# Another order of the tokens inside each 128 of the prompt, for a decoder layer with a state-space half and a gated half

## The chip, the cores and the metric

The kernel runs on one core of one Trainium2 chip. The metric is the device time of one execution in microseconds (us); the kernel before takes 1127.18 us (median of 3 runs, 1125.74 to 1130.81). Engines: TensorE (PE in the rows, PEld its weight loads), VectorE (DVE), ScalarE (ACT), GpSimd (POOL) and SyncE (SP, which only issues transfers here). Every engine works through its own list of instructions in order.

## The reference, cut to what matters

One layer for 1024 prompt tokens and 8 x 8 sample tokens (NT = 1088), width 1024:

```python
h = rmsnorm(x, norm1)
p = h @ w_in                                  # 512 columns for S5, 2 x 512 for the chunk mixer
# S5: per group of 16 channels a diagonal complex state of 64, scanned over the tokens
y = Re(C h_t) + d_skip * xf;  g = gelu(y)
o_s5 = g * sigmoid(g @ w_glu + b_glu)
# chunk mixer: inside each 128 tokens out = gelu(u) * (tril(w_s) @ layernorm(gelu(v)) + b_s)
mix = concat(rmsnorm(o_s5, g_s5), rmsnorm(o_cm, g_cm))
x = x + mix @ w_out
x = x + (silu(n @ w_gate) * (n @ w_up)) @ w_down   # n = rmsnorm(x, norm2)
y_out = rmsnorm(x, norm_f)
```

Outputs are also the last states and the normed v rows of the last chunk. All of it is in fp32.

## The kernel before, in words

Activations stand with channels on the 128 partitions and tokens along the free axis. fp32 products are made from pairs: a value x is split into a high part xh (ScalarE copies and rounds it, line 140) and a low part xl (VectorE subtracts, line 141; function `split`), and `mm3` issues three matmuls for one product. Tokens are worked in three chunks, `CH`: 384, 384 and 320 (256 of the prompt and the 64 sample tokens). The stages in time:

- **0 to 80 us**: x comes in, norm1 is summed, and `s5_in` makes the S5 input: matmuls `pu`, then line 287 multiplies them by the norm factor rB and writes them to a tile US of shape [128, 8, 136], that is [channel, t, c] where token n is c = n // 8, t = n % 8. Consecutive tokens thus lie 136 words apart: the view `tc2n` turns [p, t, c] round to [p, c, t], a step of 136 words at every element. US goes to DRAM (us_d), from where the S5 groups read it.
- **80 to 226 us**: S5, eight iterations, each with matmuls and small transfers of its state (Sw, gw, mb); between them the matmuls of the chunk mixer (`pv`, `pu`, `spt`) fill TensorE. Each iteration writes its result to DRAM (ys_d).
- **226 to 291 us**: the GLU. ys_d is read back into four tiles g ([128, 8, 136], line 742, `G5`). `s5_act` splits g into xh and xl for the matmuls (through `tc2n`: source with a step of 136 words), `glu` has matmuls `pg`, a sigmoid sg on ScalarE, the product g * sg in place on VectorE (line 762, step of 136), its square on ScalarE (lines 174 and 179) and the running sum of squares (line 180). `glu_mix` sums over the partitions with a matmul against ones (`ss`, line 158), takes the reciprocal root (`rsqrt_bc`: ScalarE line 165, VectorE lines 166 to 168), scales g (line 699) and splits it once more. It runs once per chunk; the output product `po` of the other half (the chunk mixer's) lies around it, two of the three `glu_mix` being placed behind the 6th and 11th of its 16 groups.
- **291 to 330 us**: the second half of the output product. Then the norm and the first sums of the feed-forward part, **420 to 835 us** its gate and up matrices, **835 us on** its down matrix and the last norm.

The sums `ss` have one bank of PSUM of their own (tag `sp`), so each sum waits until VectorE has read the one before with line 166. The pool `raw` has three buffers, through which all weights from DRAM go before they are split (function `load_q`, line 227); a load is issued when a buffer is free. The order of instructions on every engine is decided by a scheduler when the program is built.

Of the kernel before, what the change touches and what calls it, by code (L numbers as in the profile page):

```python
# [13 lines left out]
AF = mybir.ActivationFunctionType  # L14
# [4 lines left out]
D = 1024  # L19
# [3 lines left out]
NF = 22  # L23
CH = ((0, 384), (384, 384), (768, 320))
# [58 lines left out]
def layer_kernel(ctx: ExitStack, tc: tile.TileContext, A, O, dbg=None):  # L83
# [37 lines left out]
    def tc2n(a, n0, n):  # L121

        return a[:, :, n0 // 8:(n0 + n) // 8].rearrange("p t c -> p c t")

    def nat(a):
        return a.rearrange("p (c t) -> p c t", t=8)
# [43 lines left out]

    def accum_sq(pl, acc, src, first):

        if first:
            S.activation(acc, src, AF.Square)
            return
        sq = tmp_sq(pl, int(np.prod(src.shape[1:])), "sq")
        if len(src.shape) == 3:
            sq = nat(sq)
        S.activation(sq, src, AF.Square)
        V.tensor_tensor(acc, acc, sq, ALU.add)  # L180
# [99 lines left out]
    def s5_in(q, c):  # L280
        n0, n = CH[c]
        pp = fm_group(q, c, "s5" if c == 2 else "mm")
        for m in range(2):
            mt = 2 * q + m
            if c == 0:
                US[mt] = prep.tile([128, 8, 136], F32, tag="us", name="us", bufs=2)
            V.tensor_tensor(tc2n(US[mt], n0, n), nat(pp[m]), nat(rB[:, n0:n0 + n]), ALU.mult)  # L287
            if c == 2:
                Q.dma_start(fmaj(us_d, mt), US[mt])
# [360 lines left out]
    def cm_out(q, c):  # L650
# [3 lines left out]
        for i in range(2):  # L654
# [11 lines left out]
            for om, o, w in om_blocks(m, c):  # L666
                d = [x[:, o:o + w] for x in (p, ur, sqo[:, n0:n0 + n])]
                t_ = 128 if w > 64 else 8
                d = [x.rearrange("p (j t) -> p j t", t=t_) for x in d]
                om = om.rearrange("p (j t) -> p j t", t=t_) if w == 64 else om  # L670
                V.scalar_tensor_tensor(om, d[0], gcol("lng", m), bB[:, m:m + 1, 0:t_].to_broadcast([128, w // t_, t_]),
                                       op0=ALU.mult, op1=ALU.add)
                V.tensor_tensor(om, om, d[1], ALU.mult)
                if m == 0:
                    S.activation(d[2], om, AF.Square)
                    continue
                sq = tmp_sq(cwp, w, "sq").rearrange("p (j t) -> p j t", t=t_)
                S.activation(sq, om, AF.Square)
                V.tensor_tensor(d[2], d[2], sq, ALU.add)
# [64 lines left out]
    def s5_act(c):  # L744
        n0, n = CH[c]
        for m in range(4):
            split(tc2n(G5[m], n0, n), nat(xh[:, m, n0:n0 + n]), nat(xl[:, m, n0:n0 + n]))
# [3 lines left out]
    def glu(c):  # L751
        n0, n = CH[c]
        acc = ACC5[c] = gl.tile([128, 384], F32, tag="acc", name="acc", bufs=3)[:, :n]
        for m in range(4):
# [6 lines left out]
            z = tc2n(G5[m], n0, n)  # L761
            V.tensor_tensor(z, z, nat(sg), ALU.mult)
            accum_sq(gl, nat(acc), z, m == 0)

    def glu_mix(c):
        n0, n = CH[c]
        rb = rsqrt_bc(gl, sum_sq(ACC5[c], n), n, 1.0 / W)
        for m in range(4):
            scaled_split(tc2n(G5[m], n0, n), gcol("gs5", m), nat(rb), nat(xh[:, m, n0:n0 + n]),
                         nat(xl[:, m, n0:n0 + n]))  # L770
# [457 lines left out]

S5P = np.arange(512).reshape(4, 8, 16).transpose(0, 2, 1).reshape(-1)


def lay(inp):
# [3 lines left out]
    A = {"xT": xt.T.reshape(8, 128, NT).transpose(1, 0, 2)}  # L1236
# [33 lines left out]
    pos = np.arange(128)  # L1270
    ws, bs = one("w_s"), one("b_s")
    A["wsT"] = ws.transpose(2, 0, 1)
    tt, bb = np.tile(np.arange(8), 8), np.repeat(np.arange(8), 8)
    A["bd"] = ws[:, tt][:, :, tt].transpose(2, 0, 1)
    mk = np.zeros((128, 192), np.int32)
    mk[:, :128] = pos[:, None] <= pos[None, :]
    mk[64:, 128:] = (tt[:, None] <= tt[None, :]) & (bb[:, None] == bb[None, :])
    A["mk"] = mk
    A["bB"] = bs.reshape(4, 2, 128).transpose(1, 0, 2)
# [6 lines left out]
def unlay(R):  # L1286
    y = R["yT"].reshape(D, NT).T
# [4 lines left out]
    cvp, cvs = R["cvp"].reshape(1, 1, 128, W), R["cvs"].reshape(1, 8, 8, W)  # L1292
# [18 lines left out]
```

## Time and profile before

| | |
|---|---|
| time, median of 3 runs | 1127.18 us (1125.74 to 1130.81) |
| profiled execution: time | 1127.69 us |
| its span, granted clock of TensorE | 1125.6 us, 0.982 |
| TensorE busy, weight loads busy | 1056.9 us (94%), 1029.3 us (91%) |
| VectorE, ScalarE, GpSimd busy | 907.8 us (81%), 449.4 us (40%), 316.3 us (28%) |

The profiled execution is one run of its own; its time is 2.1 us over its span (start and end outside the profile), and it lies 0.5 us over the median of the runs. Times inside it are counted from the start of the span. TensorE is the engine with the most work, so what an edit does to the time is read from TensorE's idle stretches and from what each of them waits for.

### The profile page before, as it was taken

The numbers are of one execution on the slowest core, as the hardware profiler recorded it, in microseconds if no ns is written. First come the engines' busy times: TensorE is split into PE (matmuls) and PEld (weight loads), VectorE is DVE, ScalarE is ACT, GpSimd is POOL, SyncE is SP. The second block draws the span as 40 slices with busy tenths as digits, with TensorE's granted clock in tenths as the row PEclk, the third lists the DMA queues.
The fourth block names the chain that finished last, engine by engine and source line by source line (L and its number), as shares of the span: only waits on it lengthen the run. The fifth ranks groups of instructions, "written<-read, shape, count | busy, mean of one in ns | idle before, by whom it ended". The sixth has DMA issues, their size and how long they took to land.

```text
span 1125.6 us, 20406 instructions
## 1 busy us (share of the span) xinstructions
PE 1056.9 (94%) x7966; PEld 1029.3 (91%) x7966; DVE 907.8 (81%) x1780; ACT 449.4 (40%) x822; POOL 316.3 (28%) x287
## 2 busy tenths in 40 slices
PE   7799999978899989999999999999999999999994
PEld 6789999868799879999999999999998899899994
DVE  6987999889999897667657656657668979879998
ACT  7314334398454442232232232233234324425561
POOL 5010330000000344334334334435434331223220
PEclk9989999989899899999999999999999999999998
DMA  8342334251533113223223223133156815514304
GB/s 272 106 116 74 96 114 153 76 181 43 192 102 101 50 56 127 69 95 127 69 95 126 68 97 125 57 108 126 57 186 213 291 38 184 179 52 135 130 16 158
DMA packets 81519, 131.19 MB, mean 117 GB/s; under 512 B 8976, under 2 KB 60048, under 8 KB 81296
## 3 DMA queue, kind: packets, MB, share of 16 engines
q1 hardware_dynamic: 81424, 129.91, 35.5%
q8 instruction: 62, 1.02, 0.4%
q14 instruction: 33, 0.27, 0.1%
HBM read 90.43 MB, written 34.24 MB: 111 GB/s over the span
## 4 chain that ended last, share of the span: by engine, by line
PE 68%; DVE 19%; DMA 6%; issue 4%; ACT 3%; POOL 1%; SPq 0%; DVEq 0%; ACTq 0%; POOLq 0%
PE u L146 16%; PE u L144 16%; PE u L145 16%; DMA h<-hid_d 4%; DVE xl L141 3%; PE pu L144 2%; PE pu L146 2%; PE pu L145 2%; PE po L146 2%; PE po L144 2%; PE po L145 2%; PE pv L145 2%; PE pv L146 2%; PE pv L144 2%; DVE cwr L141 1%
## 5 line engine op out<-in xcount | busy, mean ns | idle before, releaser
L144 PE MATMUL u<-xh,h 128*128 128x272 f32 x516 | 149.5, 290 | 1.9 <-ACT h L140 1.7
L146 PE MATMUL u<-xh,h 128*128 128x272 f32 x516 | 149.1, 290 | 1.3 <-DVE h L141 1.3
L145 PE MATMUL u<-xl,h 128*128 128x272 f32 x516 | 149.0, 289 | 1.2 <-DVE xl L141 1.2
L144 PE MATMUL u<-xh,fb 128*128 128x272 f32 x382 | 110.5, 289 | 0.6 <-DVE x1r L1108 0.4
L145 PE MATMUL u<-xl,fb 128*128 128x272 f32 x382 | 110.4, 289 | 0.6 <-DVE xl L141 0.6
L146 PE MATMUL u<-xh,fb 128*128 128x272 f32 x382 | 110.3, 289 | 0.2 <-DVE fb L141 0.2
L1023 POOL TENSOR_TENSOR tS<-q,q 128x512 f32<-128x512 f32 x22 | 29.1, 1321 | 262.3 <-DVE h L888 158.4
L144 PEld LDWEIGHTS u<-xh,h 128*128 128x128 f32 x516 | 97.4, 189 | 2.7 <-ACT h L140 2.1
L146 PEld LDWEIGHTS u<-xh,h 128*128 128x128 f32 x516 | 97.4, 189 | 1.9 <-DVE h L141 1.9
L145 PEld LDWEIGHTS u<-xl,h 128*128 128x128 f32 x516 | 97.5, 189 | 1.4 <-DVE xl L141 1.4
L140 ACT ACTIVATE h<-q 128x512 fp32r<-128x512 f32 (+1 forms) x83 | 51.1, 615 | 82.0 <-PE u L145 75.8
L144 PE MATMUL pu<-xh,cwr 128*128 128x384 f32 (+1 forms) x192 | 66.4, 350 | 9.0 <-DVE us L287 9.0
L141 DVE TENSOR_TENSOR h<-q,h 128x512 fp32r<-128x512 f32 (+1 forms) x83 | 68.7, 830 | 6.4 <-ACT h L140 5.3
L145 PEld LDWEIGHTS u<-xl,fb 128*128 128x128 f32 x382 | 72.3, 189 | 1.0 <-DVE xl L141 0.9
L144 PEld LDWEIGHTS u<-xh,fb 128*128 128x128 f32 x382 | 72.2, 189 | 1.0 <-DVE x1r L1108 0.6
L146 PEld LDWEIGHTS u<-xh,fb 128*128 128x128 f32 x382 | 72.0, 189 | 0.4 <-DVE fb L141 0.4
L1061 ACT ACTIVATE st<-st 128x272 f32<-128x272 f32 x88 | 37.8, 431 | 71.2 <-DVE st L1083 35.1
L145 PE MATMUL pu<-xl,cwr 128*128 128x384 f32 (+1 forms) x192 | 65.2, 341 | 0.0
L146 PE MATMUL pu<-xh,cwr 128*128 128x384 f32 (+1 forms) x192 | 65.1, 342 | 0.0
L140 ACT ACTIVATE fb<-q 128x512 fp32r<-128x512 f32 (+1 forms) x64 | 38.7, 607 | 61.2 <-PE u L145 48.3
L1028 POOL TENSOR_TENSOR tS<-tS,q 128x512 f32<-128x512 f32 x22 | 29.8, 1354 | 114.6 <-DVE h L141 61.3
L144 PE MATMUL u<-cwr,h 128*128 128x272 f32 x189 | 55.1, 292 | 1.6 <-ACT cwr L140 1.0
(439 smaller groups left out, 3765.7 us busy)
## 6 DMA issues: line engine op xcount, KB each, us to landing
hid_d<-st SPq DMA_DIRECT2D x22, 952.0 KB, 4.2
h<-hid_d SPq DMA_DIRECT2D x28, 544.0 KB, 3.9
q<-in_w_gate_dram SPq DMA_DIRECT2D x22, 512.0 KB, 3.5
q<-in_w_up_dram SPq DMA_DIRECT2D x22, 512.0 KB, 3.5
q<-in_w_d_dram SPq DMA_DIRECT2D x16, 512.0 KB, 3.9
wo<-in_w_out_dram SPq DMA_DIRECT2D x14, 512.0 KB, 4.2
wi<-in_w_in_dram SPq DMA_DIRECT2D x12, 512.0 KB, 4.9
h<-hid_d SPq DMA_DIRECT2D x14, 408.0 KB, 3.2
```

Source lines behind the costliest of these rows:

```text
L140: S.activation(hi, src, AF.Copy)
L141: return (eng or V).tensor_tensor(lo, src, hi.bitcast(F32), ALU.subtract)
L144: PE.matmul(p, wh, ah, start=start, stop=False)
L145: PE.matmul(p, wh, al, start=False, stop=False)
L146: return PE.matmul(p, wl, ah, start=False, stop=stop)
L1023: P.tensor_tensor(tS, a21, a22, ALU.add)
L1028: P.tensor_tensor(tS, tS, a11, ALU.subtract)
L1061: S.activation(dst, src, AF.Silu)
```

## The change

Inside each 128 tokens of the prompt the order becomes t first, then c: place 16 t + c holds token 8 c + t (c from 0 to 15, t from 0 to 7). The 64 sample tokens are turned in the same way (8 x 8). With that, 16 neighbouring tokens of the free axis lie in 16 neighbouring words of a [p, t, c] tile (8 for the sample tokens). The third chunk has both kinds, so `tc2n` returns a list of pieces: one for the first two chunks, two (256 and 64 tokens) for the third. The scaling in `glu_mix` becomes one instruction per 128 tokens. Mask, spatial matrices, biases, x and the outputs are permuted on the host. Sizes and number of transfers stay.

```diff
-    def tc2n(a, n0, n):
-
-        return a[:, :, n0 // 8:(n0 + n) // 8].rearrange("p t c -> p c t")
-
-    def nat(a):
-        return a.rearrange("p (c t) -> p c t", t=8)
+    def tc2n(a, n0, n, *rest):
+
+        out = []
+        for o, w in ((0, n),) if n0 + n < NT else ((0, n - 64), (n - 64, 64)):
+            c0, cc = ((n0 + o) // 8, 16) if w > 64 else (128, 8)
+            v_ = a[:, :, c0:c0 + w // 8]
+            e = "p (j t c) -> p j t c" if w > 64 else "p (t c) -> p t c"
+            if w > 64:
+                v_ = v_.rearrange("p t (j c) -> p j t c", c=16)
+            out.append([v_] + [x[:, o:o + w].rearrange(e, t=8, c=cc) for x in rest])
+        return out
...
+    SQT = {}
+
+    def accum_to(pl, acc, first):
+
+        SQT[0] = acc if first else tmp_sq(pl, acc.shape[1], "sq")
+        return SQT[0]
+
+    def accum_end(acc, first):
+        if not first:
+            V.tensor_tensor(acc, acc, SQT[0], ALU.add)
...
-            V.tensor_tensor(tc2n(US[mt], n0, n), nat(pp[m]), nat(rB[:, n0:n0 + n]), ALU.mult)
+            for us_, p_, r_ in tc2n(US[mt], n0, n, pp[m], rB[:, n0:n0 + n]):
+                V.tensor_tensor(us_, p_, r_, ALU.mult)
...
-            split(tc2n(G5[m], n0, n), nat(xh[:, m, n0:n0 + n]), nat(xl[:, m, n0:n0 + n]))
+            for x in tc2n(G5[m], n0, n, xh[:, m, n0:n0 + n], xl[:, m, n0:n0 + n]):
+                split(*x)
...
-            z = tc2n(G5[m], n0, n)
-            V.tensor_tensor(z, z, nat(sg), ALU.mult)
-            accum_sq(gl, nat(acc), z, m == 0)
+            for z, s_, q_ in tc2n(G5[m], n0, n, sg, accum_to(gl, acc, m == 0)):
+                V.tensor_tensor(z, z, s_, ALU.mult)
+                S.activation(q_, z, AF.Square)
+            accum_end(acc, m == 0)
...
-            scaled_split(tc2n(G5[m], n0, n), gcol("gs5", m), nat(rb), nat(xh[:, m, n0:n0 + n]),
-                         nat(xl[:, m, n0:n0 + n]))
+            for x in range(0, n, 128):
+                w = min(128, n - x)
+                z = G5[m][:, :, (n0 + x) // 8:(n0 + x + w) // 8]
+                r_ = rb[:, x:x + w].rearrange("p (t c) -> p t c", t=8)
+                V.scalar_tensor_tensor(z, z, gcol("gs5", m), r_, op0=ALU.mult, op1=ALU.mult)
+            for x in tc2n(G5[m], n0, n, xh[:, m, n0:n0 + n], xl[:, m, n0:n0 + n]):
+                split(*x)
...
+CP = np.arange(128).reshape(16, 8).T.reshape(-1)
+TP = np.concatenate([(128 * np.arange(8)[:, None] + CP).reshape(-1), 1024 + np.arange(64).reshape(8, 8).T.reshape(-1)])
...
-    A = {"xT": xt.T.reshape(8, 128, NT).transpose(1, 0, 2)}
+    A = {"xT": xt[TP].T.reshape(8, 128, NT).transpose(1, 0, 2)}
...
-    A["wsT"] = ws.transpose(2, 0, 1)
+    A["wsT"] = ws[:, CP][:, :, CP].transpose(2, 0, 1)
```

Since the scheduler sees other durations, it also puts instructions elsewhere. Three places. On SP, at the end of S5: ys_d is the last result written to DRAM, g the four loads back, wo weights of the output product, x1a the residual. Before:

```order
L573 DMA ys_d<-ys 128x544
L742 DMA g_2718<-ys_d 128x8x136
L742 DMA g_2720<-ys_d 128x8x136
L742 DMA g_2722<-ys_d 128x8x136
L742 DMA g_2724<-ys_d 128x8x136
L227 DMA wo_3007<-in_w_out_dram 128x1024
```

and now (line 227 has become 242, 573 has become 589, 742 has become 761):

```order
L589 DMA ys_d<-ys 128x544
L242 DMA wo_3035<-in_w_out_dram 128x1024
L761 DMA g_2722<-ys_d 128x8x136
L761 DMA g_2724<-ys_d 128x8x136
L761 DMA g_2726<-ys_d 128x8x136
L761 DMA g_2728<-ys_d 128x8x136
L242 DMA wo_3118<-in_w_out_dram 128x1024
```

A weight load that came behind the four g loads is now ahead of them. On TensorE, at the same time: ss sums the squares of the chunk mixer's output (sqo), spt is its spatial product, yb the last S5 iteration's output and pg the first GLU product. Before:

```order
L570 MATMUL yb<-Hp,QK 128x136
L158 MATMUL ss<-sqo,ones 128x384
L664 MATMUL spt<-wT,v 64x128 x4
L664 MATMUL spt<-bd,v 64x64 x2
L158 MATMUL ss<-sqo,ones 128x384
L144 MATMUL pg<-xh,wgh 128x384 x7
```

and now:

```order
L164 MATMUL ss<-sqo,ones 128x384
L585 MATMUL yb<-U,mb_833 128x136 x2
L680 MATMUL spt<-wT,v 64x128 x4
L680 MATMUL spt<-bd,v 64x64 x2
L164 MATMUL ss<-sqo,ones 128x384
L586 MATMUL yb<-Hp,QK 128x136
```

Both sums now stand ahead of the last yb matmuls instead of behind them. On VectorE, between the reading of the first and of the second sum of `glu_mix` (rsa): g is scaled (line 699, now 794), xl is its low part, cwr a split of weights, x1a and x1q take the output product's groups. Before:

```order
L168 SCALAR_TENSOR_TENSOR rsy<-rsa,rsy 128x384
L699 SCALAR_TENSOR_TENSOR g_2718<-g_2718,gp,rsy 128x48x8
L699 SCALAR_TENSOR_TENSOR g_2720<-g_2720,gp,rsy 128x48x8
L699 SCALAR_TENSOR_TENSOR g_2722<-g_2722,gp,rsy 128x48x8
L699 SCALAR_TENSOR_TENSOR g_2724<-g_2724,gp,rsy 128x48x8
L141 TENSOR_TENSOR cwr<-wo_3170,cwr 128x1024
L141 TENSOR_TENSOR xl<-g_2718,xh 128x384
L141 TENSOR_TENSOR xl<-g_2720,xh 128x384
L141 TENSOR_TENSOR xl<-g_2722,xh 128x384
L141 TENSOR_TENSOR xl<-g_2724,xh 128x384
L166 SCALAR_TENSOR_TENSOR rsa<-ss,rsy 128x384
```

and now:

```order
L174 SCALAR_TENSOR_TENSOR rsy<-rsa,rsy 128x384
L794 SCALAR_TENSOR_TENSOR g_2722<-g_2722,gp,rsy 128x8x16 x3
L794 SCALAR_TENSOR_TENSOR g_2724<-g_2724,gp,rsy 128x8x16 x3
L794 SCALAR_TENSOR_TENSOR g_2726<-g_2726,gp,rsy 128x8x16 x3
L794 SCALAR_TENSOR_TENSOR g_2728<-g_2728,gp,rsy 128x8x16 x3
L842 TENSOR_TENSOR x1a<-x1a,po 128x272
L147 TENSOR_TENSOR cwr<-wo_3118,cwr 128x1024
L842 TENSOR_TENSOR x1q_3049<-x1q_3049,po 128x272
L147 TENSOR_TENSOR xl<-g_2722,xh 128x384
L147 TENSOR_TENSOR xl<-g_2724,xh 128x384
L842 TENSOR_TENSOR x1q_3049<-x1q_3049,po 128x272
L147 TENSOR_TENSOR xl<-g_2726,xh 128x384
```

The block of scaling and splitting was unbroken and now has the output product's additions between its parts; the scalings are twelve instead of four. The low parts of the S5 stage's filler and its matmuls also stand in another mixture, with the same work.

## Rows read from the trace of the kernel before

**Rows 1.** The page's busy time of each engine, and instructions.

```profile
PE 1056.9 (94%) x7966; PEld 1029.3 (91%) x7966; DVE 907.8 (81%) x1780; ACT 449.4 (40%) x822; POOL 316.3 (28%) x287
```

**Rows 2.** Windows: stretch, length, busy us per engine (instructions), clock, DMA share, GB/s.

```profile
80.00:226.00 146.00, 144.80 (x1111) 134.88 (x1109) 134.99 (x303) 55.02 (x126) 24.29 (x29) 1.00 0.38 108
226.00:235.00 9.00, 2.21 (x16) 1.28 (x16) 5.89 (x11) 8.06 (x10) 0.00 (x0) 0.82 1.05 291
235.00:262.00 27.00, 25.35 (x139) 24.61 (x139) 26.61 (x43) 25.71 (x39) 0.00 (x0) 0.93 0.35 123
262.00:291.00 29.00, 20.88 (x149) 19.43 (x147) 27.89 (x58) 19.95 (x33) 0.00 (x0) 0.92 0.35 115
291.00:330.00 39.00, 37.63 (x288) 37.20 (x287) 36.83 (x72) 19.14 (x30) 0.00 (x0) 0.97 0.32 108
```

**Rows 3.** TensorE's timeline; in brackets the idle time before and what ended it.

```profile
56.76 0.66 PE L144 MATMUL pu<-xh,cwr 128*128 128x384 f32 x1 [6.99 <-DVE us L287]
69.87 0.38 PE L144 MATMUL pu<-xh,cwr 128*128 128x320 f32 x1 [1.97 <-DVE us L287]
...
222.21 0.70 PE L569 MATMUL yb<-U,mb 128*128 128x136 f32 x4 [1.16 <-DMA mb<-mb]
...
234.63 2.61 PE L144 MATMUL pg<-xh,wgh 128*128 128x384 f32 x7 [2.96 <-ACT xh L140]
...
256.94 0.81 PE L158 MATMUL ss<-sqo,ones 128*128 128x320 f32 x2 [1.34 <-DVE cwf L166]
267.66 0.91 PE L158 MATMUL ss<-acc,ones 128*128 128x384 f32 x2 [1.43 <-DVE cwf L166]
277.04 0.91 PE L158 MATMUL ss<-acc,ones 128*128 128x384 f32 x2 [1.29 <-DVE rsa L166]
289.91 1.44 PE L158 MATMUL ss<-acc,ones 128*128 128x320 f32 x2 [5.40 <-DVE rsa L166]
...
319.02 0.73 PE L158 MATMUL ss<-fbt,ones 128*128 128x272 f32 x2 [1.36 <-DVE fbt L874]
```

**Rows 4.** VectorE's groups of one shape: busy us, mean ns of one, idle before.

```profile
L141 DVE TENSOR_TENSOR xl<-g,xh 128x384 fp32r<-128x384 f32 x16 | 13.6, 896 | 0.0
...
L762 DVE TENSOR_TENSOR g<-g,sg 128x384 f32<-128x384 f32 x8 | 7.4, 934 | 0.4 <-ACT sg L760 0.4
L699 DVE SCALAR_TENSOR_TENSOR g<-g,gp,rsy 128x384 f32<-128x384 f32 x8 | 7.3, 992 | 0.0
L287 DVE TENSOR_TENSOR us<-pu,rB 128x384 f32<-128x384 f32 x8 | 6.5, 905 | 2.0 <-DMA us_d<-us 2.0
...
L657 DVE TENSOR_TENSOR cwf<-pu,rB 128x384 f32<-128x384 f32 x8 | 4.4, 544 | 0.1
L141 DVE TENSOR_TENSOR xl<-v,xh 128x384 fp32r<-128x384 f32 x8 | 4.2, 557 | 0.0
...
L608 DVE SCALAR_TENSOR_TENSOR cwf<-rB,idn 128x128 f32<-128x128 f32 x9 | 2.8, 307 | 0.1
```

**Rows 5.** VectorE's timeline in `glu_mix`.

```profile
281.68 3.59 DVE L699 SCALAR_TENSOR_TENSOR g<-g,gp,rsy 128x384 f32<-128x384 f32 x4
...
289.29 0.56 DVE L166 SCALAR_TENSOR_TENSOR rsa<-ss,rsy 128x384 f32<-128x384 f32 x1
```

**Rows 6.** TensorE's timeline behind the longest idle stretch.

```profile
291.37 0.43 PE L145 MATMUL po<-xl,fb 128*128 128x272 f32 x1
...
292.96 0.41 PE L146 MATMUL po<-xh,fb 128*128 128x272 f32 x1
...
293.84 0.29 PE L146 MATMUL po<-xh,cwr 128*128 128x272 f32 x1
293.96 0.29 PE L144 MATMUL po<-xh,cwr 128*128 128x272 f32 x1
```

**Rows 7.** SP's timeline at the g loads: start, time of the four issues.

```profile
226.65 4.53 SPq L742 DMA_DIRECT2D g<-ys_d  x4
```

**Rows 8.** DMA issues: KB each, median us from issue to landing.

```profile
Sw<-Ss SPq DMA_DIRECT2D x16, 128.0 KB, 2.7
```

More of the change, by code (lines that the diff above doesn't have):

```diff
@@ L176, in accum_sq @@
         sq = tmp_sq(pl, int(np.prod(src.shape[1:])), "sq")
-        if len(src.shape) == 3:
-            sq = nat(sq)
         S.activation(sq, src, AF.Square)
@@ L670, in cm_out @@
                 om = om.rearrange("p (j t) -> p j t", t=t_) if w == 64 else om
-                V.scalar_tensor_tensor(om, d[0], gcol("lng", m), bB[:, m:m + 1, 0:t_].to_broadcast([128, w // t_, t_]),
-                                       op0=ALU.mult, op1=ALU.add)
+                if w > 64:
+                    bias = bB[:, m:m + 1, :].to_broadcast([128, w // 128, 128])
+                else:
+                    bias = bB[:, m, 0:128:16].unsqueeze(2).to_broadcast([128, 8, 8])
+                V.scalar_tensor_tensor(om, d[0], gcol("lng", m), bias, op0=ALU.mult, op1=ALU.add)
                 V.tensor_tensor(om, om, d[1], ALU.mult)
@@ L1269, in lay @@
     A["ln"] = np.stack([one("cm_ln_g"), one("cm_ln_b")])
-    pos = np.arange(128)
     ws, bs = one("w_s"), one("b_s")
-    A["wsT"] = ws.transpose(2, 0, 1)
-    tt, bb = np.tile(np.arange(8), 8), np.repeat(np.arange(8), 8)
+    A["wsT"] = ws[:, CP][:, :, CP].transpose(2, 0, 1)
+    tt, bb = np.repeat(np.arange(8), 8), np.tile(np.arange(8), 8)
     A["bd"] = ws[:, tt][:, :, tt].transpose(2, 0, 1)
     mk = np.zeros((128, 192), np.int32)
-    mk[:, :128] = pos[:, None] <= pos[None, :]
+    mk[:, :128] = CP[:, None] <= CP[None, :]
     mk[64:, 128:] = (tt[:, None] <= tt[None, :]) & (bb[:, None] == bb[None, :])
     A["mk"] = mk
-    A["bB"] = bs.reshape(4, 2, 128).transpose(1, 0, 2)
+    A["bB"] = bs[:, CP].reshape(4, 2, 128).transpose(1, 0, 2)
     return {k: np.ascontiguousarray(x) for k, x in A.items()}
@@ L1286, in unlay @@
 def unlay(R):
-    y = R["yT"].reshape(D, NT).T
+    y = np.empty((NT, D), np.float32)
+    y[TP] = R["yT"].reshape(D, NT).T
     yp, ys = y[:1024].reshape(1, 1024, D), y[1024:].reshape(8, 8, D)
@@ L1291, in unlay @@
     ss = [fs[64 * i:64 * i + 64, :, 1:].transpose(2, 1, 0)[None] for i in range(2)]
-    cvp, cvs = R["cvp"].reshape(1, 1, 128, W), R["cvs"].reshape(1, 8, 8, W)
+    cvp = R["cvp"].reshape(1, 1, 8, 16, W).transpose(0, 1, 3, 2, 4).reshape(1, 1, 128, W)
+    cvs = R["cvs"].reshape(1, 8, 8, W).transpose(0, 2, 1, 3)
     return tuple(np.ascontiguousarray(x) for x in (yp, ys, sp[0], sp[1], cvp, ss[0], ss[1], cvs))
```

## Prediction

> **What bounds the kernel now.** I read the page's busy times first. TensorE is busy 94% of the span, VectorE 81%, ScalarE 40% [rows 1]; the change takes work from VectorE and ScalarE alone, so it can only give time where TensorE stands idle for them. Where that is, the windows show: in S5 TensorE is busy 144.80 of 146.00 us, while from 235 to 291 it is busy 25.35 + 20.88 = 46.23 of 56 us and VectorE 26.61 + 27.89 = 54.50 of 56 [rows 2]. In the GLU, then, VectorE sets the pace. TensorE's timeline tells which waits these are [rows 3]. Before the pu matmuls of the first stage it stands 6.99 and 1.97 us, both ended by line 287, which writes US. From 256.94 to 289.91 four sums (ss) find their one bank still unread: 1.34, 1.43, 1.29 and 5.40 us, together 9.46, ended by VectorE's line 166 each time. The longest ends at 289.91, when VectorE reaches line 166 at 289.29 [rows 5]; ahead of it in VectorE's list lay the scaling of g (four instructions, 3.59 us), a split of weights and four low parts of g. So the instructions that the change makes cheaper are the ones that the longest wait waits for.
>
> **The price of one instruction.** Strided and unstrided forms of the same size stand side by side in VectorE's groups [rows 4]:
> - line 287 (us from pu) 905 ns, against 544 for line 657, the same product from the same kind of tile to one without steps: 0.36 less.
> - xl from g 896, against xl from v 557: 0.34 less.
> - line 762 (g times sg) 934, against the same 544: 0.39 less.
> - line 699 (scaling g) 992. It becomes three instructions of 128x128; line 608 has that shape at 307, so three are 921. But neighbours overlap: four of line 699 take 3.59 us [rows 5] and not 4 x 0.992 = 3.97, which is 0.13 less at each of three joints. Three instructions thus stand at 0.921 - 2 x 0.13 = 0.66, so 0.3 less.
>
> The third chunk (320 tokens, in two pieces) gains less, from the same rows by estimate some 0.3, 0.25, 0.3 and 0.25 (size 320/384, and one more instruction). No row shows an instruction with runs of 16 words on a side that is written; I take it to be as fast as an unstrided one, the nearest row of the same work, and keep no gain at all as the other end.
>
> [...]
>
> **The terms, in order of time.**
> 1. *First stage.* TensorE goes on at 56.76 when the first instruction of a pair of line 287 has read its bank. Ahead of it in VectorE's list stands the first pair. Three instructions at 0.36 are -1.1. Nothing, if VectorE waits there for x anyway; six at 0.36, -2.2, if all that stand before 69.87 count.
> 2. *S5 in another mixture.* The same instructions, TensorE 99% busy: 0. Between -1 (the wait of 1.16 at 222.21 goes [rows 3]) and +2.5 (two more such).
> 3. *Start of the GLU.* A weight load of 512 KB now stands ahead of the g loads on SP and needs a raw buffer that VectorE must free. At the 291 GB/s of this stretch [rows 2] its bytes take 1.8 us; its own issue, by the 4.53 us for four [rows 7], 1.1, of which I count 1.0; g is 2.8 later. Queued behind it are the four g loads, then xh, xl and the pg matmuls. Against this: the wait of 2.96 before pg ended with ScalarE's xh [rows 3] and ScalarE is busy 8.06 of 9.00 us there [rows 2], so it was not only g that was late; in the new order the sums over sqo come earlier, and ScalarE's root with them, and xh from g becomes cheaper. I take +0.5, between -1 and +2.8.
> 4. *Idle time from 256 to 291.* VectorE's saving in this stretch: eight xl of 384 at 0.34, four of 320 at 0.3, eight of line 762 at 0.39, four of 320 at 0.3, four scalings at 0.3 and four more xl at 0.34: 2.7 + 1.2 + 3.1 + 1.2 + 1.2 + 1.4 = 10.8 us. TensorE's four waits are 9.46. The saving covers them, but a sum has still to wait for the root of the one before; I leave one wait of the short kind, 1.34, and take -8.1. Bounds: -3 (the long wait shrinks by scalings and low parts of one chunk alone, 1.2 + 1.4, and little else) and -9.5. What is late next: the output product's additions on VectorE, which free TensorE's banks and now stand between the low parts.
> 5. *Clock.* [...] Without so long a wait -1.4; 0 if the wait only gets shorter by half.
> 6. *291 to 330.* Eight more scalings and eight more splits get cheaper, but TensorE is busy 37.63 of 39.00 [rows 2]; what is left is the wait of 1.36 at 319.02 [rows 3]. Half of it, -0.7; between 0 and -1.4.
>
> VectorE's added instructions are in the prices. ScalarE's second pieces (four xh, four squares, four more xh) lie beside VectorE's; if that cover were gone, 12 at the 0.06 us that one more VectorE instruction costs (worked out under the second rival) would be 0.7 us. The feed-forward part is not touched.
>
> Sum: -1.1 + 0 + 0.5 - 8.1 - 1.4 - 0.7 = -10.8. The profiled execution took 1127.7, so 1116.9; it lay 0.5 over the median of the runs, so 1116.4, and I say 1116.5. With every term at its worse bound it is 1127.7 + 2.3 = 1130, with every term at its better one 1127.7 - 16.5 = 1111.
>
> **Rivals.** What a measurement of this kernel can tell from no change is about 0.5%, 5.6 us.
> - *The idle time only moves.* TensorE works 94% of the span; the sums stop waiting, but po groups then wait for VectorE's additions, or g comes late by the whole length of the weight load and its split. Term 4 at -3 and term 5 at 0 give 1127.7 - 1.1 + 0.5 - 3 - 0.7 = 1123.4, and 1125.7 with g at +2.8. For it: VectorE stays busy 36.83 of 39 right behind. Against: from 235 to 291 weight loads take 24.61 + 19.43 = 44.04 us [rows 2], so TensorE has some 12 us free there. [...]
> - *Runs of 16 are no faster.* Then the prices stay, and VectorE has 40 more instructions (24 scalings, 4 of line 287, 4 of line 762, 8 xl). The fixed part of one, from 544 ns at 384 words and 307 at 128 [rows 4], is 0.19 us, of which 0.13 overlaps: 0.06, so 2.4 us for all, and +0.5 of term 3: 1128 to 1131, no change to be told.
> - *S5 loses its cover (slower).* Eight iterations each send their state through small transfers; one takes 2.7 us [rows 8], and now all but the last are hidden behind filler matmuls, the last costs 1.16 [rows 3]. If the other mixture leaves each iteration 2.7 us without filler, that is +21.6: 1116.9 + 21.6 = 1138. It decides from (10.8 + 5.6) / 8 = 2.05 us an iteration. Against: the amount of filler is the same and TensorE is busy 99%.
> - *More than forecast.* VectorE's saving of all stages (10.8 and some 5 in the two later `glu_mix`, 2 to 3 in the first stage) carries past 330 and shortens waits in the norm there: 1107 to 1112.
>
> **Chances.** Forecast (1112 to 1121) 0.58; more 0.13; idle time only moves (1121.5 to 1127) 0.17; runs no faster 0.05; slower 0.07. Faster by over 0.5% 0.71, within it 0.22, slower 0.07. The range from 1109 to 1125 holds the forecast, two thirds of the larger gain (0.09) and three quarters of the moved idle time (0.13): 0.80.
>
> **What would show it.** Line 287 near 0.54 us at 128x384, xl from g near 0.56, line 762's successor near 0.55: if these stay near 0.9, the second rival holds. The four sums' waits between 250 and 290 under 2 us together and no po at 0.23 us spacing: if a 5 us wait stays, term 4 is wrong. TensorE's first pg within 1 us of 234.6: if it comes after 237, term 3. A busy TensorE under 97% between 80 and 226: the S5 rival. The prediction is wrong if the idle time shows up again behind po or g, or if the norm behind 330 swallows it.

## The result and the profile after

The changed kernel takes 1117.49 us (median of 4 runs, 1114.1 to 1119.5) against 1128.41 for the kernel before (4 runs, 1125.7 to 1130.8): ratio 0.9899, 95% interval 0.9872 to 0.9926. The forecast was 1116.5 within 1109 to 1125. Run once more beside other kernels it gave 0.9887 (0.9869 to 0.9906). So it is faster by 1.0 to 1.1%, about 11 to 13 us.

The execution that was profiled is the fastest of its four, 1114.1 us, so its span is 13.3 us shorter than that of before, some 2 us more than the medians differ (10.9). The page's busy times of the changed kernel, which answer to [rows 1]:

```profile
PE 1055.7 (95%) x7966; PEld 1028.5 (92%) x7966; DVE 894.6 (80%) x1820; ACT 436.8 (39%) x834; POOL 322.3 (29%) x287
```

VectorE has 40 more instructions and is 13.2 us less busy, ScalarE 12.6 us less. Its windows, to be held against [rows 2]:

```profile
80.00:226.00 146.00, 140.59 (x1072) 130.35 (x1071) 132.14 (x294) 57.39 (x128) 28.88 (x29) 0.99 0.37 103
226.00:235.00 9.00, 3.90 (x26) 2.85 (x26) 9.00 (x19) 7.34 (x12) 0.00 (x0) 0.88 0.50 145
235.00:262.00 27.00, 25.15 (x136) 24.99 (x137) 24.75 (x60) 23.67 (x55) 0.00 (x0) 0.88 0.52 166
262.00:291.00 29.00, 29.00 (x222) 28.31 (x221) 27.43 (x77) 14.04 (x27) 0.00 (x0) 1.00 0.51 170
291.00:330.00 39.00, 39.00 (x309) 38.84 (x308) 33.59 (x84) 17.62 (x36) 0.00 (x0) 1.00 0.29 95
```

From 262 to 330 TensorE is now busy without a gap, at a granted clock of 1.00. Before that it is worse off: 140.59 us busy from 80 to 226 instead of 144.80. TensorE's timeline, with all idle stretches of over 0.8 us between 40 and 360 us:

```profile
54.67 0.66 PE L150 MATMUL pu<-xh,cwr 128*128 128x384 f32 x1 [5.25 <-DVE us L303]
67.42 0.38 PE L150 MATMUL pu<-xh,cwr 128*128 128x320 f32 x1 [0.98 <-DVE us L303]
...
223.73 0.70 PE L585 MATMUL yb<-U,mb 128*128 128x136 f32 x4 [3.35 <-DMA mb<-mb]
...
236.85 2.61 PE L150 MATMUL pg<-xh,wgh 128*128 128x384 f32 x7 [6.95 <-ACT xh L146]
```

The waits at the sums, 9.46 us together in [rows 3], are gone, and so is the one of 1.36 at 319.02. The wait for the S5 state's transfer (mb) has grown from 1.16 to 3.35. The wait of 6.95 before the first GLU product is hardly new: the kernel before stood there twice, 2.96 us in [rows 3] and, just ahead of that, 3.83 at a sum that [rows 3] leaves out:

```profile
230.76 0.91 PE L158 MATMUL ss<-sqo,ones 128*128 128x384 f32 x2 [3.83 <-DVE cwf L166]
```

That sum now stands ahead of the last yb matmuls, so the two waits (6.79 together) have become one. The first GLU product starts at 236.85 instead of 234.63, although the first stage ended earlier. SyncE's timeline there, to be held against [rows 7], and the last S5 result (ys_d) of the kernel before:

```profile
222.36 0.53 SPq L242 DMA_DIRECT2D wo<-in_w_out_dram  x1
224.61 0.34 SPq L597 DMA_DIRECT2D out_fs_dram<-fs  x1
229.51 0.32 SPq L589 DMA_DIRECT2D ys_d<-ys  x1
229.94 0.37 SPq L242 DMA_DIRECT2D wo<-in_w_out_dram  x1
230.41 5.68 SPq L761 DMA_DIRECT2D g<-ys_d  x4
```

```profile
225.89 0.32 SPq L573 DMA_DIRECT2D ys_d<-ys  x1
```

The g loads start at 230.41 instead of 226.65, 3.76 us later; 3.62 of that is that the last S5 result itself is issued at 229.51 instead of 225.89. The weight load ahead of them takes 0.47 us (229.94 to 230.41). VectorE's groups, to be held against [rows 4] (line 303 was 287, 147 was 141, 782 was 762, 794 was 699):

```profile
L794 DVE SCALAR_TENSOR_TENSOR g<-g,gp,rsy 128x128 f32<-128x128 f32 x32 | 8.9, 345 | 0.0
L147 DVE TENSOR_TENSOR xl<-g,xh 128x384 fp32r<-128x384 f32 x16 | 8.2, 551 | 0.3 <-ACT xh L146 0.2
...
L782 DVE TENSOR_TENSOR g<-g,sg 128x384 f32<-128x384 f32 x8 | 4.3, 551 | 1.5 <-ACT sg L780 1.5
L303 DVE TENSOR_TENSOR us<-pu,rB 128x384 f32<-128x384 f32 x8 | 4.1, 549 | 2.1 <-DMA us_d<-us 2.1
```

Three are at the price forecast: 549, 551 and 551 ns, as unstrided ones. The scaling is not: a third of it takes 345 ns instead of 307, and the twelve pieces of one `glu_mix` take 3.24 us where the four of before took 3.59 [rows 5], so a scaling is 0.09 us cheaper and not 0.3:

```profile
271.50 3.24 DVE L794 SCALAR_TENSOR_TENSOR g<-g,gp,rsy 128x128 f32<-128x128 f32 x12
```

For all that follows one measure is used: the first matmul of four products in TensorE's timeline. rsw comes at the end of the first stage, pg is the first GLU product, po the first of the output product, u the first of the feed-forward part. The stretch from rsw to pg is S5 and the start of the GLU, from pg to po the GLU's own products, from po to u the output product with `glu_mix` and the norm. Us, worked out from the start times (one profiled execution each):

```
kernel            first rsw   rsw to pg   pg to po   po to u
before               75.0       159.6       28.6      111.6
changed              71.0       165.8       27.0       99.3
changed, again       73.5       165.4       27.0       99.3
old_tokens           72.4       167.4       27.3      110.3
us_hop               74.4       167.3       27.4       99.3
glu_hop              73.5       164.9       27.7      111.2
mix_hop              71.8       165.4       27.3      105.3
g_first              73.3       164.0       27.4       99.3
pairs                73.1       160.4       27.3      102.2
oct                  73.5       159.3       26.5      104.0
pairs_v              72.8       160.5       26.8       99.7
pairs_vp             73.7       160.1       26.1       99.6
sum_late             73.5       165.9       26.7       99.7
sum_late_g           73.5       164.6       27.3       99.3
```

Behind u the span goes on for 749.1 to 754.5 us in these profiles: 750.8 in the kernel before, 749.1 and 752.0 in the two of the changed kernel, which are one program. So the spans of two profiles can differ by some 3 us there without any cause in the edit.

### The profile page after: what moved, and what is told of

It is laid out like the page before. It is cut to its first block, busy times and chain, and to the rows that moved or that the text cites. A ratio compares the mean times of both kernels' runs of the same rounds, so it can differ in the third digit from the quotient of the medians.

```text
span 1112.3 us, 20465 instructions
## 1 busy us (share of the span) xinstructions
PE 1055.7 (95%) x7966; PEld 1028.5 (92%) x7966; DVE 894.6 (80%) x1820; ACT 436.8 (39%) x834; POOL 322.3 (29%) x287
## 4 chain that ended last, share of the span: by engine, by line
PE 65%; DVE 18%; DMA 8%; issue 4%; ACT 3%; POOL 1%; SPq 0%; DVEq 0%; ACTq 0%; POOLq 0%
PE u L152 15%; PE u L150 15%; PE u L151 15%; DMA h<-hid_d 4%; PE po L152 3%; PE po L151 3%; PE po L150 3%; DVE xl L147 2%; PE pv L151 1%; PE pv L150 1%; PE pv L152 1%; DVE cwr L147 1%; DVE fb L147 1%; DMA gw<-gt 1%; PE pg L150 1%
```

## Experiments

The theory after the first result: the gain is the speed of the instructions on US and g, almost all of it in the GLU; the new order that the scheduler made of the changed list is a loss of some 6 us between rsw and pg. The rival: the new order, which puts the output product's additions between the low parts, took the waits at the sums away, whatever the instructions cost.

**old_tokens: the new list and order, the old token order.** The order on every engine is that of the changed kernel, instruction by instruction; only the shapes of the views differ.

```diff
-            e = "p (j t c) -> p j t c" if w > 64 else "p (t c) -> p t c"
-            if w > 64:
-                v_ = v_.rearrange("p t (j c) -> p j t c", c=16)
-            out.append([v_] + [x[:, o:o + w].rearrange(e, t=8, c=cc) for x in rest])
+            v_ = v_.rearrange("p t c -> p c t")
+            out.append([v_] + [x[:, o:o + w].rearrange("p (c t) -> p c t", t=8) for x in rest])
...
-CP = np.arange(128).reshape(16, 8).T.reshape(-1)
+CP = np.arange(128)
```

> The instruction list of the changed kernel, in exactly its order on TensorE, ScalarE, GpSimd and SyncE and the same instructions in the same order on VectorE, but with the old token order, so that every instruction on [p, t, c] steps 136 words at each element as before. It parts the two things that the change did: it keeps the new list and order and takes away the runs of 16. Theory 1 (the speed of these instructions is the whole gain, and the new order is a loss of some 3 to 6 us by the S5 stage and the start of the GLU): slower than before, 1131 to 1135, with line 303 near 0.9 us at 128x384, and waits of more than 8 us at the four sums. Rival 2 (the scheduler's new order, with the additions between the low parts, is what took the waits away): 1117 to 1122, with the sums' waits gone though the instructions are slow.

Measured: 1131.78 us, ratio to before 1.0018 (1.0006 to 1.0030). The new list and order by themselves gain nothing; they cost some 2 us. Line 303 is back at 892 ns and the scaling at 473 a third:

```profile
L147 DVE TENSOR_TENSOR xl<-g,xh 128x384 fp32r<-128x384 f32 x16 | 13.7, 895 | 0.0
L794 DVE SCALAR_TENSOR_TENSOR g<-g,gp,rsy 128x128 f32<-128x128 f32 x32 | 12.6, 473 | 0.0
L782 DVE TENSOR_TENSOR g<-g,sg 128x384 f32<-128x384 f32 x8 | 7.4, 942 | 1.3 <-ACT sg L780 1.3
L303 DVE TENSOR_TENSOR us<-pu,rB 128x384 f32<-128x384 f32 x8 | 6.5, 892 | 2.1 <-DMA us_d<-us 2.1
```

TensorE's waits of over 0.5 us between 270 and 300 us in this kernel:

```profile
275.71 0.39 PE L150 MATMUL po<-xh,cwr 128*128 128x272 f32 x1 [0.64 <-ACT sg L780]
280.10 0.91 PE L164 MATMUL ss<-acc,ones 128*128 128x384 f32 x2 [2.62 <-DVE rsa L172]
286.73 0.39 PE L150 MATMUL po<-xh,cwr 128*128 128x272 f32 x1 [1.16 <-DVE x1a L842]
292.16 0.81 PE L164 MATMUL ss<-acc,ones 128*128 128x320 f32 x2 [2.15 <-DVE rsa L172]
```

They are smaller than before (2.62 and 2.15 at sums instead of 9.46 at four), less than the over 8 us that theory 1 expected, so there is something in the rival too: with every instruction at its old speed the new order has halved these waits. But the stretch from rsw to pg is 7.8 us longer than before, at the old speed of every instruction, which takes it all back.

**us_hop and glu_hop: one part of the runs undone at a time.** The same words, walked with a step of 136 on the tile's side, by turning the last two dimensions of the views; order as in the changed kernel.

```diff
+    hop = lambda xs: [x.rearrange("p j t c -> p j c t" if len(x.shape) == 4 else "p t c -> p c t") for x in xs]
...
-            for us_, p_, r_ in tc2n(US[mt], n0, n, pp[m], rB[:, n0:n0 + n]):
+            for us_, p_, r_ in map(hop, tc2n(US[mt], n0, n, pp[m], rB[:, n0:n0 + n])):
```

> The changed kernel with one line's elements walked in the old way: line 303 (US) goes through the same words, but with a step of 136 words on the side that is written and 16 on the sides that are read; order of all instructions the same. Theory 1 (the first stage gave 4 us and they reach the end, since TensorE works on without idle time behind it): 3 to 5 us slower than the changed kernel, 1120 to 1122. Rival 2 (the S5 chain of small transfers sets the time, so that an earlier start of S5 is lost again before the GLU): within 1.5 us of the changed kernel, 1116 to 1119, with the first GLU product at the same time as in it (236.9 us).

> The other part: the changed kernel with the GLU's lines (splits of g, product with the sigmoid, square, scaling) walked with a step of 136 words on g and 16 on the other operands, US kept in runs of 16; same order of instructions. Theory 1 (most of the gain lies in VectorE's GLU work): 10 to 15 us slower than the changed kernel, 1127 to 1133, waits at the sums back. Rival 2 (the order took the waits away): within 3 us of it, up to 1120.

Measured: us_hop 1120.29 us, ratio 0.9910 (0.9893 to 0.9928), which against the changed kernel's 0.9887 and 0.9899 is 1 to 3 us. Its interval overlaps theirs, so neither expectation is settled by the total; it is small, as term 1 had it. glu_hop 1131.91 us, ratio 1.0017 (1.0005 to 1.0028): without the runs in the GLU's lines the whole gain is gone, 13 to 15 us by the ratios. Theory 1 holds there, and the waits at the second and third sum of `glu_mix` are back (2.62 and 2.10 us). The size is an upper bound, since these instructions are a little slower than in old_tokens (xl 921 ns against 895, the product 976 against 942, ScalarE's copy of g 998 against 948). And the edit slows ScalarE's copies and squares together with VectorE's lines; that VectorE sets the time is read from the waits, which end with its line 172, and no run parts the two engines.

**mix_hop: only `glu_mix` undone** (scaling and second split), the same edit on its two lines.

> The changed kernel, in its order, with glu_mix alone (scaling of g and the second splits) walked with a step of 136 words on g; s5_act, the product with the sigmoid and its square stay in runs of 16. It parts the 13 us of the GLU. Theory 1 (the waits at the sums are all VectorE's work between line 172 and line 172, so glu_mix): 6 to 10 us slower than the changed kernel, ratio 0.995 to 0.999, waits of 2 us and more at the second and third sum. Rival 2 (the whole GLU is bound by VectorE, each part gives by its share): 4 to 6 us slower, ratio 0.993 to 0.995.

Measured: 1121.48 us, ratio 0.9914 (0.9892 to 0.9935), 2 to 3 us by the ratios; its profiled execution, the slowest of its runs, has 6.0 us more from po to u. By the medians it is less than either expectation, by that profile between them. So of the 13 to 15 us `glu_mix` has 2 to 6. What the GLU's other lines would cost by themselves no run shows, so whether the parts add stays open.

**g_first: the weight load behind the g loads again.** (The scheduler then also re-sorts a part of VectorE's and ScalarE's lists and of the GLU's matmuls.)

```diff
-        Q.dma_start(g5, fmaj(ys_d, m))
+        LAST["g5"] = Q.dma_start(g5, fmaj(ys_d, m))
...
-        load_wo(1, q, q)
+        with tc.issue_after(LAST["g5"].ins) if q == 3 else ExitStack(): load_wo(1, q, q)
```

> The changed kernel with one load of output weights held behind the four g loads on SyncE, as before the change; the scheduler then also puts its split behind those of g. Theory 1 (the load ahead of g costs its issue, 0.45 us, and its 512 KB of transfer, some 1.8): first GLU product 1.5 to 2.5 us earlier than 236.9, total 1115 to 1116. Rival 2 (the last S5 result itself is late, issued at 229.5 instead of 225.9, and the load ahead costs only its issue): first GLU product at most 0.6 us earlier, total within 1 us of the changed kernel.

Measured: 1118.39 us, ratio 0.9901 (0.9884 to 0.9918), no change against the changed kernel. In the trace the stretch from rsw to pg is 164.0 instead of 165.4 and 165.8, so 1.4 to 1.8 us come back there (about theory 1's size; its total, 1115 to 1116, did not come), which the total can't tell from noise. The wait for mb (3.34) and most of that for xh stay:

```profile
225.18 0.70 PE L585 MATMUL yb<-U,mb 128*128 128x136 f32 x4 [3.34 <-DMA mb<-mb]
...
237.32 2.61 PE L150 MATMUL pg<-xh,wgh 128*128 128x384 f32 x7 [5.93 <-ACT xh L146]
```

The load ahead of g is the small part of the loss; the large one lies ahead of it.

**sum_late, sum_late_g: the sum behind the last S5 matmuls again.** In the changed kernel the second sum over sqo stands ahead of the last yb matmuls, which TensorE takes in order (in its first profile the sum starts at 225.82 and the yb matmuls behind it at 227.26); here it is put behind them, in sum_late_g with the edit of g_first as well. (The scheduler then also re-sorts a part of VectorE's and ScalarE's lists.)

```diff
-        rb = rsqrt_bc(cwp, sum_sq(sqo[:, n0:n0 + n], n), n, 1.0 / W)
+        with tc.issue_after(LAST["yb"].ins) if c == 1 else ExitStack(): ss = sum_sq(sqo[:, n0:n0 + n], n)
+        rb = rsqrt_bc(cwp, ss, n, 1.0 / W)
```

> The changed kernel with one sum of TensorE, the second over sqo, held behind the last S5 matmuls (yb), as in the kernel before; in the changed kernel it stands ahead of them and they follow 1.4 us after its start. The scheduler then puts the weight load of 512 KB ahead of the last S5 result on SyncE too. Theory 1 (in-order TensorE: the sum and the stretched matmuls ahead of yb make the last S5 result late, and with it g): last ys_d issued 1 to 2 us earlier in relation to the first rsw, rsw to pg 163 to 165 us instead of 165.4 and 165.8. Rival 2 (what makes the result late is only the exchange before, the wait of 3.35 for mb): ys_d and rsw to pg unchanged within 0.5 us.

> The same with the weight load behind the four g loads as well: both edits to the end of S5 undone. Theory 1 (each is a part of the loss, 1.4 for the sum and 1.4 to 1.8 for the load): rsw to pg 161.5 to 163.5 us; the rest of the way to 159.6 is the exchange that came late before them. Rival 2: as g_first, 164.

Measured: sum_late 1118.53 us, ratio 0.9908 (0.9883 to 0.9933), rsw to pg 165.9; sum_late_g 1117.74, ratio 0.9891 (0.9867 to 0.9916), rsw to pg 164.6. Theory 1 fell: with the sum out of the way the stretch is as long as in the changed kernel, and with both edits no shorter than with g_first alone (164.0). In sum_late the scheduler also put a weight load ahead of the last S5 result, which costs 0.43 us there; in sum_late_g there is none. In sum_late the wait for the exchange stays as it was, ahead of both:

```profile
225.88 0.99 PE L585 MATMUL yb<-U,mb 128*128 128x136 f32 x4 [3.35 <-DMA mb<-mb]
```

**after_again: the changed kernel once more.**

> The changed kernel once more, beside the others on the same chip: ratio 0.988 to 0.992. Its first stage, from run to run, tells how far the 4 us by which TensorE was earlier there in the first profile belong to the change: theory 1 (the three cheaper instructions of line 303 alone, some 1 us): first rsw matmul anywhere between 71 and 74. Rival 2 (4 us of it by the change): again at 71.

Measured: 1118.35 us, ratio 0.9887. The first rsw is at 73.5, not at 71.0. Over all kernels with line 303 at 0.55 us it lies between 71.0 and 73.7 (mean of eleven 73.0), with it at 0.9 us at 75.0, 72.4 and 74.4 (mean 73.9). So most of the 4 us in the first profile was chance; the 1 us between the means is no more than the scatter. The two waits before the pu matmuls, which line 303 ends, tell more: together they are 6.1 to 7.2 us in the eleven profiles (mean 6.9) and 7.8 to 9.0 in the three (mean 8.2), so the cheaper line gives some 1.3 us.

**pairs, oct: the old order with fast instructions.** Another token order: runs of 2 (or 8) words, by one rule for all 1088 tokens, so that the third chunk needs no second piece. The scaling, whose view would need a dimension more, becomes a product with a tile made on ScalarE.

```diff
-        return a[:, :, n0 // 8:(n0 + n) // 8].rearrange("p t c -> p c t")
+        return a[:, :, n0 // 8:(n0 + n) // 8].rearrange("p t (q c) -> p q t c", c=2)
...
-            scaled_split(tc2n(G5[m], n0, n), gcol("gs5", m), nat(rb), nat(xh[:, m, n0:n0 + n]),
-                         nat(xl[:, m, n0:n0 + n]))
+            z, rm = tc2n(G5[m], n0, n), gl.tile([128, 384], F32, tag="sg", name="rbm", bufs=2)[:, :n]
+            S.activation(rm, rb, AF.Copy, scale=gcol("gs5", m))
+            V.tensor_tensor(z, z, nat(rm), ALU.mult)
+            split(z, nat(xh[:, m, n0:n0 + n]), nat(xl[:, m, n0:n0 + n]))
```

> A token order of its own: runs of 2 words instead of 16 in the same [p, t, c] tiles, the same rule for all 1088 tokens, so that the third chunk needs no second piece and the instruction list of the kernel before stays; only the scaling of g becomes a product with a tile that ScalarE makes (rsy times the gain, 12 instructions more on ScalarE). The scheduler then puts everything up to glu_mix in exactly the order of the kernel before. Theory 1 (cheaper instructions are the gain, the new order costs 6 us between the first stage and the first GLU product): that cost goes, first GLU product 159 to 161 us after the first rsw matmul instead of 164 to 167; 2 to 6 us under the changed kernel, ratio to before 0.984 to 0.989. Rival 2 (the new order's mixing in glu_mix is needed, and the unbroken block brings the long wait at the third sum back): waits at the sums of 5 us and more, ratio 0.991 to 0.997. Rival 3 (runs of 2 are too short for the full rate): line 287 above 0.65 us at 128x384, and a ratio near 1.

> The same as the kernel with runs of 2, in the same order on every engine, with runs of 8. Theory 1 (full rate from runs of 2 on): VectorE's instructions on g and US within 2% of those with runs of 2, time within 3 us. Rival 3 (the longer the run, the faster): those with runs of 2 at least 5% slower.

Measured: pairs 1117.99 us, ratio 0.9879 (0.9859 to 0.9900); oct 1117.04, a single run. The stretch from rsw to pg is back at 160.4 and 159.3 us (before 159.6, changed 165.4 and 165.8): the loss there belongs to the order, and fast instructions don't cause it. In the total, though, pairs is no better than the changed kernel, since po to u is 102.2 (104.0 in oct) instead of 99.3. TensorE stands there once, and VectorE before it:

```profile
281.27 0.39 PE L144 MATMUL po<-xh,fb 128*128 128x272 f32 x1 [2.36 <-DVE x1q L821]
```

```profile
280.78 0.78 DVE L821 TENSOR_TENSOR x1q<-x1q,po 128x272 f32<-128x272 f32 x2 [2.38 <-DMA x1q<-in_xT_dram]
```

No sum waits; what is late is a new thing, the residual tile x1q from DRAM. Its loads are issued from 273.64 here and from 263.25 in the changed kernel; SyncE's rows, first pairs, then the changed kernel:

```profile
273.64 6.11 SPq L807 DMA_DIRECT2D x1q<-in_xT_dram  x8
```

```profile
263.25 4.59 SPq L828 DMA_DIRECT2D x1q<-in_xT_dram  x8
```

x1q lies where the chunk mixer's v was, and in the old order the last splits of v come later. So the rival's half is this: the new order is worth some 3 us behind po, by an early x1q. On VectorE the length of the runs makes no difference; its groups with runs of 2, then with runs of 8 (551, 551 and 549 with 16):

```profile
L141 DVE TENSOR_TENSOR xl<-g,xh 128x384 fp32r<-128x384 f32 x16 | 8.6, 552 | 0.0
L765 DVE TENSOR_TENSOR g<-g,sg 128x384 f32<-128x384 f32 x8 | 4.4, 561 | 0.9 <-ACT sg L763 0.9
L287 DVE TENSOR_TENSOR us<-pu,rB 128x384 f32<-128x384 f32 x8 | 4.1, 549 | 2.2 <-DMA us_d<-us 2.2
```

```profile
L141 DVE TENSOR_TENSOR xl<-g,xh 128x384 fp32r<-128x384 f32 x16 | 8.5, 549 | 0.0
L765 DVE TENSOR_TENSOR g<-g,sg 128x384 f32<-128x384 f32 x8 | 4.3, 549 | 0.3 <-ACT sg L763 0.3
L287 DVE TENSOR_TENSOR us<-pu,rB 128x384 f32<-128x384 f32 x8 | 4.1, 547 | 2.2 <-DMA us_d<-us 2.2
```

**pairs_v, pairs_vp: the old S5 order and an early x1q.** VectorE's products of the third chunk are held behind the chunk mixer's last split of v; pairs_vp makes the tile rbm on GpSimd.

```diff
-        split(src, hi, lo)
+        LAST["cm"] = split(src, hi, lo)
...
     for c in range(3):
-        glu(c)
+        with tc.issue_after(LAST["cm"].ins) if c == 2 else ExitStack(): glu(c)
```

> The kernel with runs of 2, in which VectorE stood 2.38 us for the residual tiles x1q and TensorE 2.36 us behind it, and one thing more: the product g times sg of the third chunk is held behind the chunk mixer's last split of v. The buffers of v become free earlier, and with them the loads of x1q, as in the changed kernel's own order. Theory 1 (the old order of S5 with early x1q is the better of both): the wait of 2.4 us goes, first u matmul 99 to 101 us after the first po matmul instead of 102, ratio to before 0.984 to 0.987. Rival 2 (the delay of the products makes the third sum late): a wait of 2 us and more at a sum, ratio 0.988 or above.

> The same with the tile rsy times gain made by GpSimd instead of ScalarE. Theory 1 (GpSimd idles there): the same within 2 us. Rival 2 (a GpSimd instruction of 128x384 takes over 1 us and stands between the root and the scaling): 2 to 4 us slower, VectorE waiting for rbm.

Measured: pairs_v 1114.02 us, ratio 0.9846 (0.9823 to 0.9869); pairs_vp 1116.00, ratio 0.9871 (0.9855 to 0.9888). pairs_v has both halves, 160.5 from rsw to pg and 99.7 from po to u, with x1q issued from 267.46; the wait of 2.4 us is gone. It is the fastest of all, 1.5% under the kernel before and by the ratios some 5 to 6 us under the changed one (0.9887 and 0.9899), though its interval reaches to where those of the changed kernel begin (0.9869 and 0.9872). On GpSimd rbm takes 1.4 us a piece (0.6 on ScalarE) with almost no wait for it (0.3 us in all), so rival 2's waiting VectorE isn't there; the 2 to 3 us between the two kernels can't be told from noise.

## Why the prediction was right, and where two of its terms were not

The forecast of 1116.5 is 1 us from the median. The sum behind it was -10.8. Its mechanism for the gain held, but from rsw to pg (terms 2 and 3) it was 5 to 6 us too good, from pg to u (terms 4 to 6) 3.7 us too bad, and these cancelled. That the total comes so near is in part luck.

- **Price of an instruction: right.** 0.36 less forecast for line 303, measured 905 to 549; 0.34 for xl, 896 to 551; 0.39 for the product, 934 to 551. Only the scaling was mis-sized, 0.09 instead of 0.3: its pieces are 345 ns each and not 307, so in term 4 the four scalings give 0.4 us instead of 1.2.
- **Term 1, first stage, -1.1: right in the stage itself,** some -1.3 by the two pu waits. What of it reaches the end is not settled: us_hop has 1 to 3 us, but old_tokens, where US's line is slow, and glu_hop, where it is fast, have the same total (1.0018 and 1.0017), with slightly slower GLU lines in glu_hop. The 2.1 us by which the first pu wait ends earlier in the first profile is no measure of it.
- **Terms 2 and 3, 0 and +0.5: term 2 is the step that failed.** "The same instructions, TensorE 99% busy: 0" took the S5 stage's new mixture for free. From rsw to pg the two terms together cost 5.8 to 6.2 us (159.6 to 165.4 and 165.8), just above their two upper bounds together (+2.5 and +2.8), and old_tokens and pairs show that it is the order and not the speed. The issue of the last S5 result parts them. From the first rsw to it go 158.5 and 157.6 us instead of 150.9 (in pairs and oct, with the old order, 153.0 and 151.0): term 2 is +6.7 to +7.6. From it to pg go 7.3 and 7.8 us instead of 8.7: term 3 is -0.9 to -1.4. The weight load ahead of g, the forecast's mechanism there, does cost 1.0 to 1.5 us (6.3 us without it, g_first). Against it stand the cheaper instructions (7.4 in pairs, which has the order of before) and the earlier sum, which the forecast took for a gain (7.1 without it, sum_late_g, against the 6.3; from the first rsw on 164.6 against 164.0, hardly a gain). The windows from rsw to pg, before and now, tell what TensorE lost:

```profile
75.00:234.60 159.60, 151.64 (x1162) 140.31 (x1160) 145.40 (x322) 64.03 (x139) 24.29 (x29) 0.99 0.43 121
71.00:236.90 165.90, 153.54 (x1163) 141.28 (x1161) 151.91 (x337) 67.97 (x148) 28.88 (x29) 0.98 0.41 116
```

It is idle for 12.4 us instead of 8.0, and its matmuls take 1.9 longer, at a granted clock of 0.98 instead of 0.99. The larger part of term 2 is the S5 stage's own chain of exchanges, which falls behind step by step. The start of the first gw transfer of each of the eight iterations, counted from the first rsw (SyncE's timeline, one profiled execution each):

```
before            29.3   43.8   59.5   75.9   96.6  111.8  130.8  142.4
changed           30.3   45.5   61.3   79.4  100.7  121.2  135.4  147.9
changed, again    30.0   45.1   60.9   79.0  100.3  120.8  134.9  147.0
old_tokens        30.5   45.7   61.5   79.6  100.9  121.2  135.4  147.4
pairs             29.2   43.9   59.5   76.4   97.6  113.2  131.3  143.1
```

With the new order it is 1 us late at the first, 9 at the sixth and 5 at the last, at either speed of the instructions; with the old order and fast instructions it is within 1.4 us of before. While filler matmuls are left, TensorE stands little: 2.0 us in six short pieces. When they are used up it stands 3.35 us for mb instead of 1.16, and the last S5 result comes late. Where the sixth transfer loses its time is seen in VectorE's list, first of the changed kernel, then of the kernel before. gt<-gt,CO is the first use of the fifth gw, Ss<-Ss,CO the first product of the sixth iteration and Ss<-Ss,Sw its sum; the scan makes what gw exchanges:

```profile
176.75 0.69 DVE L576 TENSOR_TENSOR gt<-gt,CO 128x512 f32<-128x512 f32 x1 [2.53 <-DMA gw<-gt]
181.48 1.21 DVE L147 TENSOR_TENSOR cwr<-wi,cwr 128x1024 fp32r<-128x1024 f32 x1
183.21 0.67 DVE L553 TENSOR_TENSOR Ss<-Ss,CO 128x512 f32<-128x512 f32 x1
187.61 0.67 DVE L555 TENSOR_TENSOR Ss<-Ss,Sw 128x512 f32<-128x512 f32 x1
190.82 1.35 DVE L559 TENSOR_TENSOR_SCAN gt<-mag,Ss 128x128 f32<-128x128 f32 x4
```

```profile
175.06 0.67 DVE L560 TENSOR_TENSOR gt<-gt,CO 128x512 f32<-128x512 f32 x1
178.71 0.67 DVE L537 TENSOR_TENSOR Ss<-Ss,CO 128x512 f32<-128x512 f32 x1
180.78 1.20 DVE L141 TENSOR_TENSOR cwr<-wi,cwr 128x1024 fp32r<-128x1024 f32 x1
182.65 0.67 DVE L539 TENSOR_TENSOR Ss<-Ss,Sw 128x512 f32<-128x512 f32 x1
185.46 1.35 DVE L543 TENSOR_TENSOR_SCAN gt<-mag,Ss 128x128 f32<-128x128 f32 x4
```

Counted from the first rsw, the fifth gw transfer is 4.1 us late, its first use 5.7 (VectorE stands 2.53 us for it), the first product of the sixth iteration 8.5, its sum 8.9 and its scan 9.4. So the largest single loss, 2.8 us, lies ahead of that product: a split of weights (cwr) and two steps of the chunk mixer now come before it and came behind it in the old order. Between sum and scan, where fillers stand in both kernels, only 0.4 us are lost.

That the order makes the chain late is shown by old_tokens and pairs; that these fillers are a part of it is read from the trace, and no run moved them alone.

- **Term 4, sums, -8.1: too small.** All 9.46 us went and no short wait stayed: TensorE is busy without a gap from 262 to 330, so no sum waits for the root of the one before, the condition given for a short wait.
- **Terms 5 and 6, clock and norm, -1.4 and -0.7: the first right, the second too small.** From 262 to 330 the granted clock is 1.00 instead of 0.92 and 0.97, and the wait of 1.36 is gone altogether. No run shows the 1.4 us of term 5 by themselves. What the traces show in their place: in the kernel before, the two sums and the nine po matmuls behind the wait of 5.40 took 3.27 us by their starts (289.91 to 293.18, the last eight po 0.23 apart), at a granted clock of 0.50; in the changed kernel the same eleven, without a wait before them, take 1.67 (281.43 to 283.10, the last eight 0.12 to 0.13 apart), at 1.00. By that some 1.6 us went, as an estimate. From pg to u, where terms 4 to 6 lie, the kernel gained 1.6 + 12.3 = 13.9 us against a forecast of 10.2. A part of what the clock gave is lost at another place: behind the wait of 6.95 the stretch from 235 to 262 runs at 0.88 instead of 0.93.
- **The rivals.** "The idle time only moves" came true in part: behind pg 11.2 us of TensorE's idle time went, and 4.4 came up between rsw and pg, not by the late weight load that the rival named. "S5 loses its cover" was the right place with the right sign and a quarter of its size (6 instead of 21.6 us); its own sign, TensorE busy under 97% from 80 to 226, came: 140.59 of 146.00 us, 96.3%. The sign for term 3, a first pg after 237, would have misled: it came at 236.85 in the first profile and at 238.93 in the second, and term 2 is why. "Runs of 16 are no faster" fell.

VectorE's rows with runs of 2, 8 and 16 words agree (549, 547 and 549 ns for US), where the step of 136 words took 905.

What stays open: why the scheduler mixes the S5 stage less well for a list that differs by second pieces and split scalings; how the GLU's gain divides between VectorE and ScalarE; and 2 to 3 us of the totals, which the noise of one profile per kernel doesn't part.

## What to carry to other kernels

When an edit changes the list of instructions, a scheduler re-sorts stages that the edit never touched; price that apart from the edit, by building the same list with the old cost of each instruction (here +2 us in total, 8 lost from rsw to pg and 2.6 given back up to u in its profile), and if it costs, look for a form of the edit that keeps the old list. On VectorE runs of two words did as well here as runs of sixteen (549 ns for US with either), and they kept the list of almost the whole kernel. And behind a wait that goes, look at once for the next load that isn't there yet, here the residual tiles, issued 10 us later with runs of two than in the changed kernel.

## What the hardware showed beside that

Stepping 136 words at each element slowed ScalarE as well as VectorE (905 ns for US against 549 in runs of 16): ScalarE's copy of g was 958 ns at 128x384 and is 519 in runs of 16, with the step on the side that is read alone:

```profile
L146 ACT ACTIVATE xh<-g 128x384 fp32r<-128x384 f32 x16 | 7.8, 519 | 3.4 <-DVE g L794 2.2 <-DMA g<-ys_d 1.2
```

Unlike VectorE (549 ns for US with runs of 2, 547 with runs of 8), ScalarE was slower with runs of 2 than with longer ones: the same copy takes 566 ns on average in pairs (534 to 613) and 513 in oct (507 to 527), which has runs of 8 and the same order on every engine.

And the first stage is not the same from run to run: in two executions of the changed kernel, one program, the first rsw matmul came at 71.0 and at 73.5 us, so a difference of 2 us there in a single pair of profiles says nothing.
